# A decoder trunk in fp32: all products of a weight's rounded part first, then those of its remainder

## The chip, the cores and the metric

The kernel runs on one core of one Trainium2 chip. The metric is the device time of the whole program in microseconds (us), as a median over runs; lower is better. All weights come from HBM during the run.

## The reference

A trunk of two decoder layers works on 256 tokens of 2048 features, in float32. In short:

```
for i in 0, 1:
    a = rmsnorm(h, attn_norm[i])
    h = h + (sb_dilated_mixer(a) if i % 2 == 0 else fox_mixer(a))     # q, k, v = a @ w_in; 16 heads of 128; @ w_out
    h = h + conv_ffn(rmsnorm(h, ffn_norm[i]))                          # u = x @ w_up (11264 wide); causal conv of width 3;
                                                                       # (silu(gate) * val) @ w_down
    gate = sigmoid(rmsnorm(h, ple_norm[i]) @ w_ple_gate[i])
    h = h + gate * (p[i] @ w_ple[i])
out = rmsnorm(h, final_norm)
```

Layer 0 mixes with 8 stick-breaking and 8 dilated-window heads, layer 1 with 16 heads with forget gates. Nearly all the arithmetic lies in the products with the weights.

## The kernel before

Features stand on the 128 partitions and tokens in the free dimension: h is a tile of 128 x 16 x 256. TensorE multiplies in a format that keeps fewer bits than float32, so that each operand is split in two: a rounded part and a remainder. An activation tile holds both for a block of 128 features, `act[:, k, 0, :]` and `act[:, k, 1, :]`, 256 columns each. A product of weight and activation is made of three partial products: rounded with rounded, rounded with remainder, remainder with rounded.

Two of them share the weight's rounded part, and are one matmul of 512 columns, called *wide* here: the weight block of 128 x 128 is loaded (LDWEIGHTS, the row PEld of the profile) and both parts of the activation stream through it (L207). The third is a *narrow* matmul of 256 columns with the block of the weight's remainder (L209). The wide one fills `ps[:, j]`, a bank of PSUM with two halves; the narrow one adds to the second half. When all k are done, `joined` (L263, L264) or `add_to_h` adds the halves.

A weight is cut into pieces, four blocks of 128 rows by 256 columns in most. One transfer of the SP queue brings two pieces (L149). ScalarE casts a piece into the rounded part (L165), and VectorE subtracts to get the remainder (L166); a call of `unit` sees to it that three pieces are split ahead of use. The split pieces lie in four buffers w. `gemm_unit` takes one piece: for each half j of its 256 columns and each k it issues wide, narrow, wide, narrow. `gemm_v` does the same for the values v, with the roles of weight and activation exchanged: the activation's block is loaded, and the weight's two parts stream (L242 wide, L244 narrow).

Some products do not follow this pattern: `flat` ones (p @ w_ple, named psp, L203), the values of the first head pair of layer 1 together with its forget gates (L256), and the last pair of gate outputs (L734). They issue narrow products alone, three for each k.

The program is written in the order of the layers: for each of eight pairs of heads the tiles psq, psk and psv; then the output projection (pso); the up projections in pairs (psu) and, in three blocks, the down projection (psd); then the gates (psg). PSUM has two tiles for these. Work of attention, norms and convolution is put among the pieces: `defer` holds it back by a number of pieces. A scheduler then orders each engine's instructions, mostly as written; the engines wait for one another by semaphores. `staggered` lets the first two pairs of outputs wait with their last piece, so that the last activations may come late.

Of the kernel before, what the change touches and what calls it, by code (L numbers as in the profile page):

```python
# [48 lines left out]


def _stagger(pairs):
    """The first two pairs end together, so that their last inputs may come late."""
    a, b = pairs[0], pairs[1]
    return sum([a[:-1], b[:-1], a[-1:], b[-1:]] + pairs[2:], [])

# [3 lines left out]


def _units():
    """Pieces of the weights, in the order in which they are used."""
    full = _cuts(KT)
    ple = [[("w_ple", l, 0, 2, c * 256, 256) for c in range(8)] for l in range(DEPTH)]
    out = list(ple[0])
    for l in range(DEPTH):
        for hp in range(NH // 2):
            if l % 2 == 1 and hp == 0:
                out += [("w_vf", l, k0, kc, 2 * D, 256 + NH) for k0, kc in VF_CUTS]
            for part in range(3):  # L70
                if l % 2 == 0 or hp > 0 or part < 2:
                    out += _pair("w_in", l, part * D + hp * 256, 0, full)
            if l > 0:
                out.append(ple[l][hp])
        out += _stagger([_pair("w_out", l, op * 256, 0, full) for op in range(8)])
        for g0, g1 in BLOCKS:
            for g in range(g0, g1):
                for half in range(2):
                    out += _pair("w_up", l, half * FF + g * 256, 0, full)
            out += _stagger([_pair("w_down", l, op * 256, 2 * g0, _cuts(2 * (g1 - g0))) for op in range(8)])  # L80
        for op in range(8):
            out += _pair("w_ple_gate", l, op * 256, 0, full)
    return out


def _groups(units):
    """Pieces that one transfer brings."""
    out, i = [], 0
    while i < len(units):
        room = 512 if i < 2 else 1024 if i < 12 else 2048  # L90
        n, size = 0, 0
        while i + n < len(units) and size + units[i + n][3] * units[i + n][5] <= room:
            size += units[i + n][3] * units[i + n][5]
            n += 1
        out.append(units[i:i + n])
        i += n
    return out
# [7 lines left out]
def trunk(ctx: ExitStack, tc: tile.TileContext, xT, pT, pos, gains, conv, bf, cst, wst, out):  # L105
    nc = tc.nc
# [30 lines left out]
    def t3_tile(name, shape=(P, 768), dt=F32):  # L137
        return work.tile(list(shape), dt, name=name, tag="t3", bufs=4)

# [1 line left out]
    raws, ready = [], []  # L141
    at = {"group": 0, "off": 0, "unit": 0, "tick": 0, "rows": 0}

# [32 lines left out]
        assert (u[0], u[1], u[2], u[4]) == (kind, l, k0, c0), (u, kind, l, k0, c0)  # L176
        return u[3], w

    # what waits for other engines is given to TensorE some pieces later
    later = []  # L180

    def defer(n, fn):
# [9 lines left out]
            due[0][1]()  # L192

    def gemm_unit(ps, act, kind, l, c0, k0, first, last, koff=0, flat=False):
        """ps[:, j, 0] and ps[:, j, 1] sum to W[:, 128 columns]^T A^T."""
        kc, w = unit(kind, l, k0, c0)
        for j in range(2):
            js = slice(j * P, (j + 1) * P)
            for k in range(kc):
                a = act[:, k0 - koff + k]  # L200
                if flat:
                    for n, (s, t) in enumerate(((0, 0), (0, 1), (1, 0))):
                        nc.tensor.matmul(ps[:, j, 0, :], lhsT=w[:, k, s, js], rhs=a[:, t, :],  # L203
                                         start=first and k == 0 and n == 0,
                                         stop=last and k == kc - 1 and n == 2)
                    continue
                nc.tensor.matmul(ps[:, j], lhsT=w[:, k, 0, js], rhs=a,  # L207
                                 start=first and k == 0, stop=False, skip_group_check=True)
                nc.tensor.matmul(ps[:, j, 1, :], lhsT=w[:, k, 1, js], rhs=a[:, 0, :],  # L209
                                 start=False, stop=last and k == kc - 1, skip_group_check=True)  # L210
        tick()

# [5 lines left out]
            k0 += kc  # L218

    def staggered(name, act, kind, l, cuts, done, k0=0, koff=0):  # L220
        """All pairs of outputs; the first two end together."""
        n = len(cuts)
        ps = [mm_tile(name) for _ in range(2)]
        for part in (range(n - 1), (n - 1,)):
            for op in range(2):
                gemm(ps[op], act, kind, l, op * 256, cuts, k0, koff, part)
                if part == (n - 1,):
                    done(op, ps[op])
        for op in range(2, 8):
            p = mm_tile(name)  # L230
            gemm(p, act, kind, l, op * 256, cuts, k0, koff)
            done(op, p)

    def gemm_v(ps, act, l, c0):
        """ps[:, t, 0] and ps[:, t, 1] sum to A[tokens of tile t] W[:, 256 columns]."""
        for i in range(4):
            kc, w = unit("w_in", l, 4 * i, c0)
            for t in range(2):
                tsl = slice(t * P, (t + 1) * P)
                for k in range(kc):  # L240
                    a = act[:, 4 * i + k]
                    nc.tensor.matmul(ps[:, t], lhsT=a[:, 0, tsl], rhs=w[:, k],  # L242
                                     start=i == 0 and k == 0, stop=False, skip_group_check=True)
                    nc.tensor.matmul(ps[:, t, 1, :], lhsT=a[:, 1, tsl], rhs=w[:, k, 0, :],  # L244
                                     start=False, stop=i == 3 and k == kc - 1, skip_group_check=True)
            tick()

    def gemm_vf(ps, act, l):
        """The same with the columns of the forget gates, all in ps[:, t]."""
        n = 256 + NH  # L250
        for k0, kc in VF_CUTS:
            _, w = unit("w_vf", l, k0, 2 * D)
            for t in range(2):
                for k in range(kc):
                    for i, (a, b) in enumerate(((0, 0), (0, 1), (1, 0))):
                        nc.tensor.matmul(ps[:, t, :n], lhsT=act[:, k0 + k, a, t * P:(t + 1) * P],  # L256
                                         rhs=w[:, k, b, :], start=k0 + k + i == 0,
                                         stop=k0 + k == KT - 1 and i == 2)
            tick()
# [12 lines left out]
        nc.vector.tensor_add(out=hs, in0=hs, in1=t)  # L272

    def parts(dst, src):
        """src as the sum of two parts that TensorE takes whole."""
        nc.scalar.copy(out=dst[:, :, 0, :], in_=src)
        nc.vector.tensor_sub(out=dst[:, :, 1, :], in0=src, in1=dst[:, :, 0, :].bitcast(F32))

# [1 line left out]
    def norm_parts(op, g, dst):  # L280
        """h pair op is final: its parts, with the gains."""
        for j in range(2):
            k = 2 * op + j
            nc.scalar.activation(out=dst[:, k, 0, :], in_=h[:, k, :], func=AF.Copy,
                                 scale=gn[:, g, k:k + 1])
            nc.vector.scalar_tensor_tensor(
                out=dst[:, k, 1, :], in0=h[:, k, :], scalar=gn[:, g, k:k + 1],
                in1=dst[:, k, 0, :].bitcast(F32), op0=ALU.mult, op1=ALU.subtract)
# [8 lines left out]
            nc.vector.tensor_add(out=acc, in0=acc, in1=sq)  # L297

    def norm_sums(more=()):
        """Reciprocal roots of the mean squares, one token a partition."""  # L300
        ps = at_tile("nps")
        nc.vector.tensor_add(out=acc[:, 0, :], in0=acc[:, 0, :], in1=acc[:, 1, :])
        rows = [acc[:, 0, :], *more]
# [18 lines left out]
                                           op0=ALU.add, op1=ALU.mult)  # L322

    def norm_rows(mixer):
        """The same, one token a column, in every partition."""
        dg = t2_tile("nd", (P, 2, P))
        ps = at_tile("rps")
        for t in range(2):
# [18 lines left out]
        defer(5, lambda: norm_rows(mixer))  # L347

    def with_rows(fn):
        """fn reads rb: not before norm_rows."""  # L350
        if at["rows"] > at["tick"]:
            later.append((at["rows"], fn))
        else:
            fn()
# [1 line left out]
    rb2 = rb.unsqueeze(1).to_broadcast([P, 2, S])  # L356
    rq2 = rq.unsqueeze(1).to_broadcast([P, 2, S])

# [1 line left out]
    def load_p(l):  # L360
        raw = t2_tile("pr")
        nc.sync.dma_start(out=raw, in_=pT[:, l])
        return raw

    def ple_up(l, op):
        """A pair of p W_ple, kept until its gates are there."""
        ps = at_tile("psp").rearrange("p j (a s) -> p j a s", a=2) if l > 0 else mm_tile("psp")
        gemm(ps, pact, "w_ple", l, op * 256, (2,), flat=True)
        nc.scalar.copy(out=pl[:, 2 * op:2 * op + 2, :], in_=ps[:, :, 0, :])
# [29 lines left out]
        nc.gpsimd.dma_start(out=bft, in_=bf)  # L399
        nc.gpsimd.dma_start(out=cv, in_=conv)  # L400

# [1 line left out]
    rc = cpool.tile([32, S], F32, name="rc")  # L403
    rs = cpool.tile([32, S], F32, name="rs")

# [30 lines left out]
        nc.vector.tensor_mul(out=x[:32], in0=x[:32], in1=rc.unsqueeze(1).to_broadcast([32, 2, S]))  # L436
        nc.vector.tensor_add(out=x[:32], in0=x[:32], in1=sw)

# [1 line left out]
    def sb_first(q, k):  # L440
        sc = at_tile("scs")
        for j in range(2):
# [75 lines left out]
        return pe, s  # L518

    def sm_second(pe, s):  # L520
        """The weights, one key a partition."""
        sp = at_tile("sps")
        for j in range(2):
            for i in range(3):
# [14 lines left out]
                             skip_group_check=True)  # L539
        parts(dst[:, 2 * hp:2 * hp + 2], av[:, 0, :].rearrange("p (j s) -> p j s", j=2))  # L540

# [1 line left out]
    def forget_gates(l, ps):  # L543
        c2 = cpool.tile([64, S], F32R, name=f"c2_{l}")
        sel = cpool.tile([64, NH], F32R, name=f"sel_{l}")
# [104 lines left out]
        nc.vector.tensor_mul(out=c[0], in0=c[0], in1=c[1])  # L650
        parts(hid[:, 2 * (g - g0):2 * (g - g0) + 2], c[0])

# [1 line left out]
    X, Y = bufs  # L654
    for l in range(DEPTH):
        st = {}
# [179 lines left out]
```

## Time and profile before

| what | value |
|---|---|
| median of 3 runs | 2520.75 us (2520.5 to 2521.31) |
| span of the profiled execution | 2519.2 us |
| TensorE products (PE) | 2497.2 us busy, 14270 instructions |
| weight loads (PEld) | 2173.1 us busy, 14270 instructions |
| VectorE (DVE) | 1716.3 us busy |
| ScalarE (ACT) | 1319.4 us busy |
| read from HBM | 452.86 MB, 181 GB/s over the span |

The profile is of one execution; its span is from the first to the last instruction, and no other time of that execution is given. PE rows are products, PEld rows the loads of their weights, which overlap products. A product's duration in the profile reaches to its modelled end, and neighbours overlap; the distance from one start to the next says what a product costs in a stream. In a row of a group, the number after x counts instructions, then follow busy time in us, the mean of one in ns, and the idle time of the engine just before them. In a row of the timeline stand the start and the duration in us, then engine, line and tiles.

### The profile page before, as it was taken

The numbers are of one execution on the slowest core, as the hardware profiler recorded it, in microseconds if no ns is written. First come the engines' busy times: TensorE is split into PE (matmuls) and PEld (weight loads), VectorE is DVE, ScalarE is ACT, GpSimd is POOL, SyncE is SP. The second block draws the span as 40 slices with busy tenths as digits, with TensorE's granted clock in tenths as the row PEclk, the third lists the DMA queues.
The fourth block names the chain that finished last, engine by engine and source line by source line (L and its number), as shares of the span: only waits on it lengthen the run. The fifth ranks groups of instructions, "written<-read, shape, count | busy, mean of one in ns | idle before, by whom it ended". The sixth has DMA issues, their size and how long they took to land. (4 is left out here: it accounts for less than half of the span.)

```text
span 2519.2 us, 34810 instructions
## 1 busy us (share of the span) xinstructions
PE 2497.2 (99%) x14270; PEld 2173.1 (86%) x14270; DVE 1716.3 (68%) x2386; ACT 1319.4 (52%) x1747; POOL 2.5 (0%) x8
## 2 busy tenths in 40 slices
PE   8999999999999999999999999999999999999997
PEld 7888888888888888888888888888888888888887
DVE  7767667776567657777765555677765776677676
ACT  6554455554455445555554444555544554455564
POOL 0000000000000000000000000000000000000000
PEclk9999999999999999999999999999999999999999
DMA  7444455555555555555454444555555555555553
GB/s 259 167 168 167 167 184 184 185 184 192 183 193 184 180 188 184 190 181 199 170 179 163 163 161 165 183 192 184 187 184 184 187 184 186 193 187 180 182 191 117
DMA packets 66431, 457.20 MB, mean 181 GB/s; under 512 B 7408, under 2 KB 7424, under 8 KB 16608
## 3 DMA queue, kind: packets, MB, share of 16 engines
q1 hardware_dynamic: 66096, 454.53, 50.5%
q8 instruction: 111, 1.82, 0.3%
q0 software_dynamic: 176, 0.46, 0.1%
q14 instruction: 48, 0.39, 0.0%
HBM read 452.86 MB, written 2.10 MB: 181 GB/s over the span
## 5 line engine op out<-in xcount | busy, mean ns | idle before, releaser
L166 DVE TENSOR_TENSOR w<-wr,w 128x1024 fp32r<-128x1024 f32 (+2 forms) x882 | 1049.8, 1191 | 532.3 <-ACT w L165 529.9
L165 ACT CAST w<-wr 128x1024 fp32r<-128x1024 f32 (+2 forms) x882 | 903.4, 1025 | 710.6 <-PE psd L209 186.7
L207 PE MATMUL psu<-act,w 128*128 128x512 f32 x2816 | 995.5, 397 | 0.0
L209 PE MATMUL psu<-act,w 128*128 128x256 f32 x2816 | 791.3, 281 | 0.0
L207 PEld LDWEIGHTS psu<-act,w 128*128 128x128 f32 x2816 | 529.4, 188 | 130.6
L209 PEld LDWEIGHTS psu<-act,w 128*128 128x128 f32 x2816 | 528.6, 188 | 0.0
L207 PE MATMUL psd<-act,w 128*128 128x512 f32 x1408 | 497.8, 397 | 0.0
L209 PE MATMUL psd<-act,w 128*128 128x256 f32 x1408 | 395.6, 281 | 0.0
L207 PEld LDWEIGHTS psd<-act,w 128*128 128x128 f32 x1408 | 264.7, 188 | 65.3
L209 PEld LDWEIGHTS psd<-act,w 128*128 128x128 f32 x1408 | 264.3, 188 | 0.0
L207 PE MATMUL psq<-act,w 128*128 128x512 f32 x512 | 183.9, 400 | 0.0
L207 PE MATMUL psk<-act,w 128*128 128x512 f32 x512 | 182.8, 399 | 0.0
L207 PE MATMUL pso<-act,w 128*128 128x512 f32 x512 | 181.5, 398 | 0.0
L242 PE MATMUL psv<-w,act 128*128 128x512 f32 x480 | 172.5, 399 | 0.7 <-DVE jn L264 0.7
L207 PE MATMUL psg<-act,w 128*128 128x512 f32 x480 | 170.0, 398 | 0.0
L209 PE MATMUL psq<-act,w 128*128 128x256 f32 x512 | 143.9, 281 | 0.7 <-DVE w L166 0.7
L209 PE MATMUL psk<-act,w 128*128 128x256 f32 x512 | 143.9, 281 | 0.0
L209 PE MATMUL pso<-act,w 128*128 128x256 f32 x512 | 143.9, 281 | 0.0
L244 PE MATMUL psv<-w,act 128*128 128x256 f32 x480 | 135.2, 282 | 0.0
L209 PE MATMUL psg<-act,w 128*128 128x256 f32 x480 | 134.9, 281 | 0.0
L263 ACT COPY jn<-psu 128x512 f32<-128x512 f32 x88 | 51.7, 588 | 147.0 <-PE psu L209 147.0
L264 DVE TENSOR_TENSOR jn<-jn,psu 128x512 f32<-128x512 f32 x88 | 60.5, 688 | 93.0 <-ACT jn L263 93.0
(202 smaller groups left out, 2317.0 us busy)
## 6 DMA issues: line engine op xcount, KB each, us to landing
wr<-in_w SPq DMA_DIRECT2D x388, 1024.0 KB, 4.8
wr<-in_w SPq DMA_DIRECT2D x36, 768.0 KB, 4.3
wr<-in_w SPq DMA_DIRECT2D x8, 896.0 KB, 4.6
wr<-in_w SPq DMA_DIRECT2D x7, 512.0 KB, 5.1
h<-in_x SPq DMA_DIRECT2D x4, 512.0 KB, 7.2
out_dram<-h SPq DMA_DIRECT2D x8, 256.0 KB, 2.4
wr<-in_w SPq DMA_DIRECT2D x2, 816.0 KB, 4.7
ct<-in_c SPq DMA_DIRECT2D x1, 841.0 KB, 6.6
```

Of the source, the lines that this page charges most:

```text
L165: nc.scalar.copy(out=w[:, :, 0, :], in_=raw)
L166: nc.vector.tensor_sub(out=w[:, :, 1, :], in0=raw, in1=w[:, :, 0, :].bitcast(F32))
L207: nc.tensor.matmul(ps[:, j], lhsT=w[:, k, 0, js], rhs=a, start=first and k == 0, stop=False, skip_group_check=True)
L209: nc.tensor.matmul(ps[:, j, 1, :], lhsT=w[:, k, 1, js], rhs=a[:, 0, :], start=False, stop=last and k == kc - 1, skip_group_check=True)
L242: nc.tensor.matmul(ps[:, t], lhsT=a[:, 0, tsl], rhs=w[:, k], start=i == 0 and k == 0, stop=False, skip_group_check=True)
L244: nc.tensor.matmul(ps[:, t, 1, :], lhsT=a[:, 1, tsl], rhs=w[:, k, 0, :], start=False, stop=i == 3 and k == kc - 1, skip_group_check=True)
L263: nc.scalar.copy(out=t, in_=ps[:, :, 1, :])
L264: nc.vector.tensor_add(out=t, in0=t, in1=ps[:, :, 0, :])
```

## The change

In `gemm_unit` and in `gemm_v` the loop over k is run twice for each half j of a piece: once for the wide products, once for the narrow ones. Every product stays, with its operands; `start` is still on the first wide product and `stop` on the last narrow one. The flat products keep their order. Comments and docstrings are dropped as well, which moves the lines' numbers by two behind this place.

```diff
         for j in range(2):
             js = slice(j * P, (j + 1) * P)
-            for k in range(kc):
-                a = act[:, k0 - koff + k]
-                if flat:
+            if flat:
+                for k in range(kc):
+                    a = act[:, k0 - koff + k]
                     for n, (s, t) in enumerate(((0, 0), (0, 1), (1, 0))):
...
-                    continue
-                nc.tensor.matmul(ps[:, j], lhsT=w[:, k, 0, js], rhs=a,
+                continue
+            for k in range(kc):
+                nc.tensor.matmul(ps[:, j], lhsT=w[:, k, 0, js], rhs=act[:, k0 - koff + k],
                                  start=first and k == 0, stop=False, skip_group_check=True)
-                nc.tensor.matmul(ps[:, j, 1, :], lhsT=w[:, k, 1, js], rhs=a[:, 0, :],
+            for k in range(kc):
+                nc.tensor.matmul(ps[:, j, 1, :], lhsT=w[:, k, 1, js], rhs=act[:, k0 - koff + k, 0, :],
                                  start=False, stop=last and k == kc - 1, skip_group_check=True)
...
                 for k in range(kc):
-                    a = act[:, 4 * i + k]
-                    nc.tensor.matmul(ps[:, t], lhsT=a[:, 0, tsl], rhs=w[:, k],
+                    nc.tensor.matmul(ps[:, t], lhsT=act[:, 4 * i + k, 0, tsl], rhs=w[:, k],
                                      start=i == 0 and k == 0, stop=False, skip_group_check=True)
-                    nc.tensor.matmul(ps[:, t, 1, :], lhsT=a[:, 1, tsl], rhs=w[:, k, 0, :],
+                for k in range(kc):
+                    nc.tensor.matmul(ps[:, t, 1, :], lhsT=act[:, 4 * i + k, 1, tsl], rhs=w[:, k, 0, :],
                                      start=False, stop=i == 3 and k == kc - 1, skip_group_check=True)
```

On TensorE, one half (128 columns) of a piece of the first query projection (psq) stood like this before, wide and narrow in turn; the numbers behind the names are those of buffers, and the waits are for ScalarE's rounded part and VectorE's remainder:

```order
L207 MATMUL psq_289<-act0_68,w_313 128x512 [waits Activation_49]
L209 MATMUL psq_289<-act0_68,w_313 128x256 [waits DVE_49]
L207 MATMUL psq_289<-act0_68,w_313 128x512
L209 MATMUL psq_289<-act0_68,w_313 128x256
L207 MATMUL psq_289<-act0_68,w_313 128x512
L209 MATMUL psq_289<-act0_68,w_313 128x256
L207 MATMUL psq_289<-act0_68,w_313 128x512
L209 MATMUL psq_289<-act0_68,w_313 128x256
```

The same piece, both halves, with the change:

```order
L208 MATMUL psq_289<-act0_68,w_313 128x512 [waits Activation_49]
L208 MATMUL psq_289<-act0_68,w_313 128x512 x3
L211 MATMUL psq_289<-act0_68,w_313 128x256 [waits DVE_49]
L211 MATMUL psq_289<-act0_68,w_313 128x256 x3
L208 MATMUL psq_289<-act0_68,w_313 128x512 x4
L211 MATMUL psq_289<-act0_68,w_313 128x256 x4
```

The wait for the remainder (DVE) has moved behind three more wide products.

At the start of the program the order of VectorE is touched too, around the first head pair, where the factors of the first norm (rT, then rb and rq) are made for the sums of psq and psk (jn). Before:

```order
L321 SCALAR_TENSOR_TENSOR rT<-nt,ny 128x2 [waits DVE_49]
L166 TENSOR_TENSOR w<-wr,w 128x4x256 [waits Activation_49]
L329 TENSOR_SCALAR nd<-ct,rT 128x128 [waits DVE_49]
L329 TENSOR_SCALAR nd<-ct,rT 128x128
L337 TENSOR_TENSOR ndl<-nd,ndh 128x256 [waits Activation_49]
L340 COPY rb<-rps 128x256 [waits PE_49]
L166 TENSOR_TENSOR w<-wr,w 128x4x256 [waits DMAHW2_49,Activation_49]
L342 TENSOR_SCALAR rq<-rb 128x256 [waits DVE_49]
L264 TENSOR_TENSOR jn<-jn,psq 128x512 [waits Activation_49]
```

With the change:

```order
L323 SCALAR_TENSOR_TENSOR rT<-nt,ny 128x2 [waits DVE_49]
L331 TENSOR_SCALAR nd<-ct,rT 128x128 [waits DVE_49]
L331 TENSOR_SCALAR nd<-ct,rT 128x128
L166 TENSOR_TENSOR w<-wr,w 128x4x256 [waits DMAHW2_49,Activation_49]
L339 TENSOR_TENSOR ndl<-nd,ndh 128x256 [waits Activation_49]
L266 TENSOR_TENSOR jn<-jn,psq 128x512 [waits Activation_49]
L342 COPY rb<-rps 128x256 [waits PE_49]
L266 TENSOR_TENSOR jn<-jn,psk 128x512 [waits Activation_49]
L344 TENSOR_SCALAR rq<-rb 128x256 [waits DVE_49]
```

The first of the two splits (L166) has moved up into the chain that makes rT, the second stands ahead of ndl, and the sum of psq is now made before rb and rq. TensorE's own product for rb (rps, L339 before, L341 now) has moved towards the end of psk. Outside this stretch the other engines' orders are unchanged.

## The prediction

> **What bounds the kernel now.** I read the page's busy table first, then its costliest groups, then the waits of TensorE, then the timeline of a steady stretch.
>
> ```profile
> span 2519.2 us, 34810 instructions
> PE 2497.2 (99%) x14270; PEld 2173.1 (86%) x14270; DVE 1716.3 (68%) x2386; ACT 1319.4 (52%) x1747; POOL 2.5 (0%) x8
> PEclk9999999999999999999999999999999999999999
> L207 PE MATMUL psu<-act,w 128*128 128x512 f32 x2816 | 995.5, 397 | 0.0
> L209 PE MATMUL psu<-act,w 128*128 128x256 f32 x2816 | 791.3, 281 | 0.0
> L207 PEld LDWEIGHTS psu<-act,w 128*128 128x128 f32 x2816 | 529.4, 188 | 130.6
> ...
> L242 PE MATMUL psv<-w,act 128*128 128x512 f32 x480 | 172.5, 399 | 0.7 <-DVE jn L264 0.7
> ```
>
> TensorE is busy for 99% of the span at full granted clock, and the two products of the large weights (L207, wide, 512 columns; L209, narrow, 256 columns) show no idle time ahead of them. Nothing but TensorE's own pace sets the end. What it does wait for is short, and all at the two ends of the program:
>
> ```profile
> PE psp L203 <- ACT w L165: 5.9, 2, 5.4
> PE rps L331 <- DVE nd L329: 2.7, 1, 2.7
> PE nps L306 <- DVE sq L745: 1.6, 1, 1.6
> PE psp L203 <- ACT pl L369: 1.4, 2, 1.3
> PE psq L209 <- DVE w L166: 0.7, 1, 0.7
> PE psv L242 <- DVE jn L264: 0.7, 1, 0.7
> ```
>
> These are microseconds in total, times, and the longest. Only the last two, 0.7 us each, touch lines that the change touches. So the question is what a step of TensorE takes from one start to the next, not the modelled durations of 397 and 281 ns, which overlap. The timeline shows the starts:
>
> ```profile
> 999.83 0.40 PE L207 MATMUL psu<-act,w 128*128 128x512 f32 x1
> 1000.07 0.28 PE L209 MATMUL psu<-act,w 128*128 128x256 f32 x1
> 1000.07 0.19 PEld L207 LDWEIGHTS psu<-act,w 128*128 128x128 f32 x1
> 1000.18 0.40 PE L207 MATMUL psu<-act,w 128*128 128x512 f32 x1
> ...
> 1007.96 0.40 PE L207 MATMUL psu<-act,w 128*128 128x512 f32 x1
> ```
>
> From 999.83 to 1007.96 there are 23 pairs of a wide and a narrow product: 8.13 / 23 = 0.3535 us a pair. Within a pair about 0.235 us go from the wide to the narrow one and 0.118 from the narrow to the next wide one: 0.46 ns a column in both. The pairs number 2816 + 1408 + 3 x 512 + 480 = 6240 (psu, psd, psq, psk, pso, psg) and 480 of psv: 6720 x 0.3535 = 2376 us of the 2519.
>
> **The change, part by part.** No product, load, byte or column is added or removed. In each half piece four pairs become four wide products and then four narrow ones. So of every four wide-to-narrow steps three become wide-to-wide, and of every four narrow-to-wide steps three become narrow-to-narrow. Over the program that is 0.75 x 6720 = 5040 steps of each new kind. A nanosecond on one of them is 5 us, which is also 0.2% of 2520.75 us, about what a measurement of this kernel can tell from no change. Everything hangs on these two prices.
>
> Narrow to narrow is in the trace. The last pair of gate outputs (L734) is two runs of 48 narrow products each, and the input projection of layer 1 (psp, L203) has runs of 12:
>
> ```profile
> 2492.20 5.65 PE pse L734 x48
> 2497.86 5.67 PE psg L734 x48
> 1290.53 1.41 PE psp L203 x12
> 1332.91 1.36 PE psp L203 x12
> ```
>
> These rows are from the chain of waits (start, us). 5.65 / 48 = 0.1177 and 5.67 / 48 = 0.1181 us a step: what narrow-to-wide takes. The psp runs give 0.1175 and 0.1133. I take 0.1177 against 0.118: 5040 x -0.0003 = -1.5 us. Bounds: 0.1181 (+0.5 us) and 0.1133 (5040 x -0.0047 = -24 us).
>
> Wide to wide is not in the trace. The nearest rows say whether a wide product's 0.235 us is its own or due to the narrow one behind it. It can be read where something else follows:
>
> ```profile
> 36.86 0.40 PE L207 MATMUL psk<-act,w 128*128 128x512 f32 x1
> 37.09 0.48 PE L306 MATMUL nps<-ct,acc 128*128 128x2 f32 x3
> ...
> 423.07 0.28 PE L209 MATMUL psu<-act,w 128*128 128x256 f32 x1
> 423.07 0.53 PEld L306 LDWEIGHTS nps<-ct,acc 128*128 128x128 f32 x4
> 423.19 0.50 PE L306 MATMUL nps<-ct,acc 128*128 128x2 f32 x4
> 423.52 0.19 PEld L207 LDWEIGHTS psu<-act,w 128*128 128x128 f32 x1
> ```
>
> Behind a wide product a product of two columns starts 0.23 us later, and behind a narrow one 0.12 us later: the same as in the pairs. So the time belongs to the product in front and its columns, whatever follows, and I take 0.235 us for wide to wide: 0 us. Bounds: twice the fastest narrow step, 2 x 0.1133 = 0.2267 (5040 x -0.0083 = -42 us), and, upwards, 1 ns a step for what no row shows (+5 us).
>
> Do the weights come in time? In the pairs a load starts with the product ahead of it and is recorded for 188 ns, longer than a narrow step; so loads overlap one another, and what counts is how close they can follow. The rows at 423.07 show four loads and then the next at 423.52: 0.45 / 4 = 0.112 us a load, below 0.118. Four narrow products in a row ask for one load each 0.118 us, so the loads stay hidden; if they did not, see the second rival.
>
> A rule of the Trainium skill gives smaller steps. "TensorE: Matmul & The Clock Gate", section "Back-to-back issue gap", puts an isolated step at N / 2.4 + 2.5 ns: 216 and 109 ns, 325 a pair. The trace has 353.5 and disagrees by 28 ns; an estimate by that page for both kinds of new step is 5040 x (-19 - 9) ns = -141 us. That would be right only if alternating were what costs the 28 ns, and the runs of L734 speak against it for the narrow half.
>
> The rest of a piece keeps its dates. Each half piece still ends with the narrow product of its last k, so its sum is ready and its weight buffer free when they were. The activations of the later k are read earlier by up to 3 x 0.118 = 0.35 us. The closest case that I found is the last head pair of layer 0, whose remainder is written just ahead of its use in the output projection:
>
> ```profile
> 339.50 0.68 DVE L277 TENSOR_TENSOR act<-avp,act 128x512 fp32r<-128x512 f32 x1
> 341.21 0.40 PE L207 MATMUL pso<-act,w 128*128 128x512 f32 x1
> ```
>
> It is done at 340.18; the piece starts at 341.21 and needs it from its third k on, 2 x 0.353 later before and 2 x 0.235 later now: 1.5 us of lead are left of 1.7. Cost 0; without that cover it would be 0.24 us, once.
>
> **The start.** Two waits move. The first is for a late remainder of a weight:
>
> ```profile
> 28.85 0.40 PE L207 MATMUL psq<-act,w 128*128 128x512 f32 x1
> 29.94 0.38 PE L209 MATMUL psq<-act,w 128*128 128x256 f32 x1 [0.69 <-DVE w L166]
> ...
> 47.47 0.28 PE L209 MATMUL psk<-act,w 128*128 128x256 f32 x1
> 48.41 0.47 PE L242 MATMUL psv<-w,act 128*128 128x512 f32 x1 [0.66 <-DVE jn L264]
> ```
>
> The step from 28.85 takes 1.09 us instead of 0.235, 0.85 too long. Three wide products now go in between, 0.70 us, so 0.15 us of the wait is left. The second, at 48.41 (0.94 instead of 0.118, 0.82 too long), is for the sum of psq, which VectorE joins only after the row factors rb. In the new order VectorE joins psq ahead of rb and rq, but the chain that makes rT and nd, which stands ahead of it, has one split of a weight (L166, 1.2 us) put into it. Queued behind the join are rb, rq and the join of psk, none of which TensorE needs before the scores of this head pair, 16 pairs on. What the first wait gives back, TensorE arrives earlier here, so I do not add them: the two together are worth between -1.7 us (both gone) and +0.8 us (the second grows by one split, about 1.2 us, while the first gives 0.4). I take -0.5.
>
> **Sum.** -1.5 + 0 + 0 - 0.5 = -2 us on the profiled span of 2519.2 us; the median of the runs, 2520.75, lies 1.6 us above that span, and I carry this difference over: 2518.75, say 2519 us.
>
> **Rivals.** *Alternating costs something* (faster). Going from one width to the other disturbs the stream, and runs of one width go at the pace of the fastest psp run. Price: -24 - 42 = -66 us, 2455 us. For it: that run, at 0.1133. Against it: L734 keeps 0.1177 over 96 products of one width, another psp run 0.1175, and a wide product takes 0.23 us in front of a two-column one. By the page's formula it would be the 2380 us of the estimate above. It decides from 1 ns a step. Chance 0.14, most of it between the ends.
>
> *The weight loads bind in the narrow half* (slower). In pairs a load behind a narrow product is followed by a long wide one in which the loads catch up; four narrow ones in a row have no such rest. If loads of different blocks cannot follow closer than, say, 0.125 us, a narrow step grows by 7 ns: 5040 x 0.007 = +35 us, 2556 us; if each took its recorded 188 ns, 5040 x 0.070 = +353 us, 2874 us. For it: in L734 two of three neighbouring loads bring the same block, so that run does not prove the pace for different blocks. Against it: the 0.112 us of L306. It decides from a load pace above 0.118. Chance 0.09.
>
> *The scheduler undoes it.* The built order shows the grouping in every piece, so this is out, but for the products of the attention and norms, which stand among the pieces as before.
>
> **How the numbers follow.** No measurable change: 0.77, with its own range of 2515.7 to 2523. Faster 0.14, slower 0.09. The range must hold 0.8, so it takes in the near part of both rivals: 2509 (a gain of 2 ns on each wide-to-wide step) to 2529 (2 ns lost on each narrow step).
>
> **What would show it.** In the timeline of the changed kernel eight products of a half piece should take 1.41 us from the first wide one to the first wide one of the next half, with wide starts 0.235 and narrow starts 0.118 us apart. PEld should stay without waits that hold TensorE. The wait of psq's first narrow product for w should shrink to 0.2 us or vanish. A wide step of 0.23 or less, or a narrow one above 0.12, proves the forecast wrong, and the size gives the time at 5 us a nanosecond.

## The result and the profile after

The changed kernel takes 2477.5 us (median of 4 runs, 2476.15 to 2478.58) against 2520.62 us before. The ratio is 0.983 with a 95% interval of 0.981 to 0.984: 43 us or 1.7% faster. The forecast was 2519 us, no measurable change, with a range of 2509 to 2529.

The page of the changed kernel, its busy table and the groups that answer to those shown of before (L208 is the wide product now, L211 the narrow one):

```profile
span 2474.4 us, 34810 instructions
PE 2453.4 (99%) x14270; PEld 2145.1 (87%) x14270; DVE 1715.1 (69%) x2386; ACT 1320.2 (53%) x1747; POOL 2.5 (0%) x8
PEclk9999999999999999999999999999999999999998
L208 PE MATMUL psu<-act,w 128*128 128x512 f32 x2816 | 767.9, 394 | 0.0
L211 PE MATMUL psu<-act,w 128*128 128x256 f32 x2816 | 437.3, 277 | 0.0
```

Instructions, granted clock and the share of TensorE are as before, and the products still have no idle time ahead of them. TensorE does the same products in less time. One stretch of the up and down projections of layer 0, 600 to 700 us, by TensorE's instructions in it, first before, then after (us, busy, in brackets the count, clock, DMA share, GB/s):

```profile
600.00:700.00 100.00, 100.00 (x568) 1.00 0.53 190
```

```profile
600.00:700.00 100.00, 100.00 (x579) 1.00 0.53 189
```

579 against 568 products in the same time is 1.9% more, in a stretch that waits for nothing. The timeline after, start and duration in us:

```profile
1000.85 1.09 PE L208 MATMUL psu<-act,w 128*128 128x512 f32 x4
1001.78 0.62 PE L211 MATMUL psu<-act,w 128*128 128x256 f32 x4
1002.24 0.62 PE L208 MATMUL psu<-act,w 128*128 128x512 f32 x2
```

From the first wide product of one half piece to that of the next go 1.39 us, 0.93 for the wide and 0.46 for the narrow ones. Before, four pairs took 4 x 0.3535 = 1.41 us. The starts of the products with the large weights in the two traces give the steps; some fifty in each kernel are longer than 260 ns and are left out:

| step from one start to the next, mean ns | before | after |
|---|---|---|
| wide to wide | none | 230.9 |
| wide to narrow | 234.8 | 235.1 |
| narrow to narrow | 117.8 (94 steps, the two runs of L734 alone) | 115.3 |
| narrow to wide | 118.5 | 113.7 |

In most half pieces of the changed kernel, those of four blocks in `gemm_unit`, the four wide steps are near 226, 236, 231 and 236 ns, and the four narrow ones 118.5 and three times 113.4. Four pairs were 4 x 353.3 = 1413 ns and are 1387: 26 ns, 1680 times, is 44 us. That accounts for the gain. The start gives about 1 us: the step that waits for the late remainder takes 0.49 us where it took 1.09, and the one that waits for psq's sum 0.47 where it took 0.94. The first wait is gone from the list of waits, and the second has shrunk from 0.7 us to this:

```profile
PE psv L243 <- DVE jn L266: 0.2, 1, 0.2
```

One place shows more than the sum. The last pair of gate outputs (L734 before, L736 now) was not touched. Its two runs of 48 narrow products, in the chain of waits after:

```profile
2447.77 5.44 PE pse L736 x48
2453.21 5.46 PE psg L736 x48
```

They took 5.65 and 5.67 us before. The same instructions on the same tiles in the same order step at 113.3 ns where they stepped at 117.7, and only what ran ahead of them differs. So a narrow product has no price of its own here: there is a *fast pace*, 113.3 ns for 256 columns, and a *slow pace*, 117.7. The experiments ask what moves the stream from one to the other. "Lines of pse" below means these two runs: they tell at which pace the stream was left.

### The profile page after: what moved, and what is told of

It reads as the page before. It is cut to its first block, busy times and chain, and to the rows that moved or that the text cites. A ratio compares the mean times of both kernels' runs of the same rounds, so it can differ in the third digit from the quotient of the medians.

```text
span 2474.4 us, 34810 instructions
## 1 busy us (share of the span) xinstructions
PE 2453.4 (99%) x14270; PEld 2145.1 (87%) x14270; DVE 1715.1 (69%) x2386; ACT 1320.2 (53%) x1747; POOL 2.5 (0%) x8
## 5 line engine op out<-in xcount | busy, mean ns | idle before, releaser
L166 DVE TENSOR_TENSOR w<-wr,w 128x1024 fp32r<-128x1024 f32 (+2 forms) x882 | 1049.2, 1191 | 500.0 <-ACT w L165 497.8
L208 PE MATMUL psu<-act,w 128*128 128x512 f32 x2816 | 767.9, 394 | 0.0
L208 PEld LDWEIGHTS psu<-act,w 128*128 128x128 f32 x2816 | 476.7, 188 | 59.9
L211 PEld LDWEIGHTS psu<-act,w 128*128 128x128 f32 x2816 | 428.2, 188 | 63.8
L211 PE MATMUL psu<-act,w 128*128 128x256 f32 x2816 | 437.3, 277 | 0.0
L208 PE MATMUL psd<-act,w 128*128 128x512 f32 x1408 | 388.8, 394 | 0.0
L208 PEld LDWEIGHTS psd<-act,w 128*128 128x128 f32 x1408 | 236.4, 188 | 26.7
L211 PEld LDWEIGHTS psd<-act,w 128*128 128x128 f32 x1408 | 219.1, 188 | 34.7
L211 PE MATMUL psd<-act,w 128*128 128x256 f32 x1408 | 224.6, 278 | 0.0
L208 PE MATMUL psq<-act,w 128*128 128x512 f32 x512 | 141.6, 398 | 0.0
L208 PE MATMUL psk<-act,w 128*128 128x512 f32 x512 | 140.9, 396 | 0.0
L208 PE MATMUL pso<-act,w 128*128 128x512 f32 x512 | 140.0, 395 | 0.0
L208 PE MATMUL psg<-act,w 128*128 128x512 f32 x480 | 131.1, 395 | 0.0
L208 PEld LDWEIGHTS psq<-act,w 128*128 128x128 f32 x512 | 86.9, 188 | 11.5 <-issue 0.2
L208 PEld LDWEIGHTS psk<-act,w 128*128 128x128 f32 x512 | 86.8, 188 | 11.2
L208 PEld LDWEIGHTS pso<-act,w 128*128 128x128 f32 x512 | 86.7, 188 | 11.0
L243 PEld LDWEIGHTS psv<-w,act 128*128 128x128 f32 x480 | 81.7, 188 | 11.8 <-PE psk L211 0.4
L208 PEld LDWEIGHTS psg<-act,w 128*128 128x128 f32 x480 | 81.3, 188 | 10.2
```

Source lines behind the costliest of these rows:

```text
L166: nc.vector.tensor_sub(out=w[:, :, 1, :], in0=raw, in1=w[:, :, 0, :].bitcast(F32))
L208: nc.tensor.matmul(ps[:, j], lhsT=w[:, k, 0, js], rhs=act[:, k0 - koff + k], start=first and k == 0, stop=False, skip_group_check=True)
L211: nc.tensor.matmul(ps[:, j, 1, :], lhsT=w[:, k, 1, js], rhs=act[:, k0 - koff + k, 0, :], start=False, stop=last and k == kc - 1, skip_grou ...
L243: nc.tensor.matmul(ps[:, t], lhsT=act[:, 4 * i + k, 0, tsl], rhs=w[:, k], start=i == 0 and k == 0, stop=False, skip_group_check=True)
```

## The experiments

All kernels start from the kernel before, unless another is named, and all edits are made in `gemm_unit` and `gemm_v` alike where the text doesn't say otherwise; the diffs show `gemm_unit`, and brackets in them stand for code that is left out. Times of single runs are set beside the run of before on the same chip.

**Does the gain follow the number of changes of width? e1_groups2, e2_groups8.** Groups of two, and of eight.

```diff
+            for ka in range(0, kc, 2):                 # e1_groups2
+                for k in range(ka, min(ka + 2, kc)):
                     (wide product of k)
+                for k in range(ka, min(ka + 2, kc)):
                     (narrow product of k)
```

```diff
+            for j in range(2):                         # e2_groups8
+                for k in range(kc):
                     (wide product of j, k)
+            for j in range(2):
+                for k in range(kc):
                     (narrow product of j, k)
```

> Groups of two: wide, wide, narrow, narrow for each two k, in both gemm_unit and gemm_v. A theory 'changes of width cost': the trace of before has 353.3 ns a pair with one wide-narrow-wide change per pair, the changed kernel 346.8 ns with a quarter; on a straight line that is 344.6 + 8.7 ns per change, so half a change per pair gives 349.0 ns a pair, 29 us under before: 2491 us. Theory 'addresses' (a product costs more when its neighbour reads the same activation block): no neighbours of the same k are left, so all of the gain is there: 2477 us. Theory 'two paces' (a stream locks onto 113.3 or 117.8 ns per 256 columns by its history): anything from 2455 to 2520, not on the line.

> Groups of eight: both halves' wide products of a piece, then both halves' narrow ones. 'Changes of width cost': an eighth of a change per pair, 345.7 ns, 51 us under before: 2469 us. 'Addresses': as the changed kernel, 2477 us. 'Two paces': between 2430 and 2520; the second half of a wide run repeats the steps of the first half (about 231 ns on average), then also near 2477 us.

Measured: 2480.05 and 2478.85 us, before 2520.23. Groups of two, four (2477.5) and eight lie within 2.6 us of one another; the straight line over the number of changes, which asked for 2491 and 2469, falls. The timeline of groups of two and of eight:

```profile
1000.32 0.62 PE L209 MATMUL psu<-act,w 128*128 128x512 f32 x2
1000.78 0.39 PE L212 MATMUL psu<-act,w 128*128 128x256 f32 x2
1001.02 0.62 PE L209 MATMUL psu<-act,w 128*128 128x512 f32 x2
```

```profile
1001.02 2.02 PE L211 MATMUL psu<-act,w 128*128 128x512 f32 x8
1002.88 1.07 PE L216 MATMUL psu<-act,w 128*128 128x256 f32 x8
1003.79 1.56 PE L211 MATMUL psu<-act,w 128*128 128x512 f32 x6
```

In groups of two, two pairs take 0.70 us; the steps are 226, 236, 118.5, 113.4. In groups of eight 16 products take 2.77 us, 0.346 a pair. The wide run goes 226, 236, 231, 236, 230.5, 236, 231, 236, and the narrow one 118.5 and seven times 113.4. So a longer run saves on narrow products (only the first is slow) and loses the same on wide ones (only the first is fast).

**Is it the neighbour that reads the same activation block? e3_shift.**

```diff
             for k in range(kc):
+                m = (k + kc // 2) % kc
                 (wide product of k)
-                (narrow product of k)
+                (narrow product of m)
```

> Wide and narrow in turn as before, but each narrow product is of another k than the wide one ahead of it (k shifted by half a piece). Same number of changes of width as before, but no neighbours that read the same activation block. 'Changes of width cost' and 'two paces' (same sequence of lengths): 353.3 ns a pair, 2520 us. 'Addresses': the gain of the change, about 2477 us.

Measured: 2522.87 us, before 2520.23; wide steps of 235 and narrow ones of 118.4 ns, 5.65 us in the lines of pse. The shared block is out: wide and narrow in turn are as slow where neighbours read different blocks.

**No wide products at all. e4_allnarrow, e8_allnarrow_timed.**

```diff
-                nc.tensor.matmul(ps[:, j], lhsT=w[:, k, 0, js], rhs=a, ...)
+                nc.tensor.matmul(ps[:, j, 0, :], lhsT=w[:, k, 0, js], rhs=a[:, 0, :], ...)
+                nc.tensor.matmul(ps[:, j, 1, :], lhsT=w[:, k, 0, js], rhs=a[:, 1, :], ...)
                 (narrow product of k)
```

> Every wide product is made as two narrow ones, so that all products with the large weights are narrow, three for each k; 6720 products and loads more, no change of width. 'Changes of width cost': three steps of 113.3 ns, 340 ns for what a pair did, 90 us under before: 2431 us. 'Addresses' (neighbours of one k are back): three steps of 117.8 ns, 353.4: 2520 us. 'Two paces': either of the two, or a mixture. If the loads bind, more than 2520 us.

> The kernel of e4_allnarrow again, timed in three rounds: 2439.7 us in one run, so a ratio of 0.968 to before and 0.985 to the changed kernel; the interval should exclude both 1 and the changed kernel's 0.983.

Measured: 2439.7 us in one run, and 2437.9 us (2437.21 to 2439.72) when timed, before 2520.37: ratio 0.967, interval 0.966 to 0.969. It beats both kernels. The page of e4_allnarrow, and TensorE's instructions in the stretch from 600 to 700 us:

```profile
span 2437.9 us, 48251 instructions
PE 2415.5 (99%) x20990; PEld 2402.3 (99%) x20990; DVE 1715.4 (70%) x2386; ACT 1323.8 (54%) x1747; POOL 2.5 (0%) x8
...
600.00:700.00 100.00, 100.00 (x884) 1.00 0.54 191
```

100 us / 884 = 113.1 ns a step. Three of them are 340 ns for what a pair did in 353.3. It issues 6720 products and loads more, the loads are busy for 99% of the span, and it is still the fastest. These products write the same halves of PSUM in the same order as the kernel before and read the same blocks. So what is slow in the kernel before is neither the blocks nor the halves of PSUM: it comes with the 512 columns in one instruction, between narrow products.

**What a wide product costs in a run of its own kind. e5_allwide.**

```diff
-                nc.tensor.matmul(ps[:, j, 1, :], lhsT=w[:, k, 1, js], rhs=a[:, 0, :], ...)
+                nc.tensor.matmul(ps[:, j], lhsT=w[:, k, 1, js], rhs=a, ...)
```

> The narrow product of the weight's remainder is made wide too (it takes both parts of the activation, so the product of the two remainders is added to the sum): wide products only, two for each k, as many loads as before. Theory 'a wide product behind a wide one pays' (runs of eight showed 231 and 236 ns in turn): 233.4 ns a step, 467 ns a pair, 763 us over before: 3283 us. Theory 'only a change of width pays': 226.7 ns a step, 453 ns a pair, 3194 us.

Measured: 3277.7 us. The steps are 233.1 ns on average, in places 231 and 236 in turn, in places 233 throughout. A wide product among its like costs 6.4 ns more than two narrow ones at the fast pace, and 1.7 ns less than in turn with narrow ones. Behind such a run the lines of pse are fast (5.45).

**Do the loads do it? e6_load64, e11_narrow64.** In `gemm_unit` alone, wide and narrow in turn, and all narrow:

```diff
+                m = P if (first and k == 0) or (last and k == kc - 1) else P // 2
+                ms = slice(j * P, j * P + m)
-                nc.tensor.matmul(ps[:, j], lhsT=w[:, k, 0, js], rhs=a, ...)
+                nc.tensor.matmul(ps[:m, j], lhsT=w[:, k, 0, ms], rhs=a, ...)
                 (the other products likewise)
```

> Wide and narrow in turn as before, but in gemm_unit all products except the first and the last of a sum load and fill only 64 of the weight block's 128 columns (half of each output's features are left out there); the streams keep their 512 and 256 columns. If the loads take time from the streams or hold them up, the pair falls from 353.3 towards 340 ns (three times the best 113.3) or below: 73 us under before or more, 2448 us or less. If the streams set the pace alone, 353.3 ns and 2520 us.

> All products narrow as in e4_allnarrow, but in gemm_unit all except the first and the last k of a sum load and fill only 64 of the weight block's 128 columns (half of each output's features are left out there). If the loads bind the narrow run, the step falls below 113.3 ns, to what the stream of 256 columns takes by itself: 108 to 110 ns, about 2360 to 2390 us. If the stream binds, 113.3 ns and 2440 us.

Measured: 2483.58 us in turn, before 2519.65, and 2443.54 us all narrow, before 2520.37. The loads of half the columns, in the kernel with both widths in turn:

```profile
1000.07 0.19 PEld L211 LDWEIGHTS psu<-act,w 128*128 128x128 f32 x1
1000.30 0.14 PEld L209 LDWEIGHTS psu<-act,w 128*64 128x64 f32 x1
1000.42 0.13 PEld L211 LDWEIGHTS psu<-act,w 128*64 128x64 f32 x1
```

In turn, the wide step falls from 235 to 228 ns and the narrow one stays at 119: neither of the two theories' numbers, but what the edit shortens does have a part in what a wide product costs. It has one in the pace too. The lines of pse behind this order, in the chain of waits of e6_load64, are fast:

```profile
2455.22 5.44 PE pse L736 x48
2460.66 5.46 PE psg L736 x48
```

So with loads of 64 columns, wide and narrow in turn do not leave the stream on the slow pace: 228 and 119 ns are close to what the first wide and the first narrow product of a group take (226 and 118.5). The edit halves the loads and, with them, the partitions of PSUM that are filled; no run tells the two apart.

All narrow, the step stays at 113.3 ns: at the fast pace the load does not set it. A load falls from 188 to 134 ns, 54 ns for 64 columns; the Trainium skill, "TensorE: Matmul & The Clock Gate", section "LDWEIGHTS (loading the stationary operand)", counts a column as 1 / 1.2 ns, 53 ns for 64, and the trace agrees in this difference. By the same rule a whole load of 128 columns is an estimated 107 ns, and the rows have 188.

**And how close can loads follow? e7_third128.** From e4_allnarrow, in `gemm_unit`:

```diff
-                (third product, 256 columns)
+                c = S if last and k == kc - 1 else S // 2
+                nc.tensor.matmul(ps[:, j, 1, :c], lhsT=w[:, k, 1, js], rhs=act[:, k0 - koff + k, 0, :c], ...)
```

> All products narrow as in e4_allnarrow, but in gemm_unit the third one, of the weight's remainder, takes only 128 of 256 columns (the rest of that product is left out, except in the last k). If the step of 113.3 ns in a narrow run is the pace of the loads, the third step stays near 112 ns: about 2432 us. If it is the pace of the stream, it falls to 57 ns: about 2110 us.

Measured: 2492.28 us, more than with the whole product. Both theories missed:

```profile
1000.04 0.34 PE L208 MATMUL psu<-act,w 128*128 128x256 f32 x1
1000.21 0.28 PE L210 MATMUL psu<-act,w 128*128 128x256 f32 x1
1000.33 0.22 PE L213 MATMUL psu<-act,w 128*128 128x128 f32 x1
1000.39 0.33 PE L208 MATMUL psu<-act,w 128*128 128x256 f32 x1
```

The short step takes 0.06 us, as the theory of the stream had it, but the step behind it 0.17. The loads in the same stretch:

```profile
1000.22 0.19 PEld L213 LDWEIGHTS psu<-act,w 128*128 128x128 f32 x1
1000.33 0.19 PEld L208 LDWEIGHTS psu<-act,w 128*128 128x128 f32 x1
1000.44 0.19 PEld L210 LDWEIGHTS psu<-act,w 128*128 128x128 f32 x1
1000.56 0.19 PEld L213 LDWEIGHTS psu<-act,w 128*128 128x128 f32 x1
```

They start 0.11 to 0.12 us apart, also where the short product stands between, so that what it saves is lost again in the next step. That this step waits for a load is read from the distances; no wait is recorded. Three loads take 0.346 us, 0.115 each. So the narrow run at 113.3 ns is near the closest spacing of loads of 128 columns seen here (0.108 us at the least in this stream of psu), and a shorter stream buys nothing. The lines of pse are slow (5.65) behind this order.

**Is the pace handed on? e10_one_pair.** The grouped order in one pair of gate outputs only:

```diff
+            if kind == "w_ple_gate" and l == 1 and c0 == 6 * 256:
+                (all wide products of the half piece, then all narrow ones)
+                continue
```

> The kernel before, with the grouped order only in the pair of gate outputs of layer 1 that stands ahead of the last two runs of 48 narrow products. Time: 1.3 us less at most, 2519 us. What it is for is the pace of those runs: 117.8 ns a step in before (5.65 us for 48), 113.3 in the changed kernel (5.44), by the same instructions. Theory 'the pace is handed on by what ran ahead': 113.3, 5.44 us. Theory 'the pace comes from the run itself, or from its place': 117.8, 5.65 us.

Measured: 2519.65 us, as before on that chip. The lines of pse:

```profile
2490.84 5.44 PE pse L742 x48
2496.28 5.46 PE psg L742 x48
```

Fast. The pace is handed on: 64 products in the grouped order, right ahead, and 96 untouched narrow products behind them go at 113.3 ns instead of 117.7, to the last one.

**What puts the stream on the slow pace, and what brings it back? e9_every_second, e12_one_wide, e13_two_wide.** All narrow, but with a wide product left in every second k, in the first k of a half piece, and in the first two k together:

```diff
             for k in range(kc):                        # from e4_allnarrow
+                if k % 2 == 0:                         # e12_one_wide: if k == 0
+                    (wide product of k)
+                else:
                     (two narrow products of k in its place)
                 (narrow product of the remainder of k)
```

```diff
+            for k in (0, 1):                           # e13_two_wide
+                (wide product of k)
+            for k in (0, 1):
+                (narrow product of the remainder of k)
+            for k in range(2, kc):
                 (three narrow products of k)
```

> For every second k the wide product is made as two narrow ones, so that each wide product stands between narrow ones: wide, narrow, narrow, narrow, narrow. Theory 'the pace is handed on': a wide product behind narrow ones at the fast pace takes 226.5 ns, the narrow one behind it 118.4, the other three 113.4 each: 685 ns for two pairs' work, 2448 us. Theory 'every change of width costs alike' (13.3 ns in before for wide-narrow-wide): 2 x 340 + 13.3 = 693 ns, 2476 us.

> In each half piece only the first k keeps its wide product; the other k have three narrow ones: one wide and ten narrow products in a row (for four k). Theory 'a lone wide product puts the stream on the slow pace, and narrow ones keep what they find': 235.3 + 10 x 117.7 = 1412 ns a half piece, 2517 us. Theory 'a wide product costs some nanoseconds near it only': 4 x 340 + 13 = 1373 ns, 2452 us.

> In each half piece the first two k have wide, wide, narrow, narrow, the other two three narrow products each: two wide and eight narrow in a row. Theory 'two wide products in a row bring the stream back to the fast pace': 226 + 236 + 118.4 + 7 x 113.4 = 1374 ns a half piece, 2456 us. Theory 'any wide product among narrow ones spoils them': 2 x 235.5 + 8 x 117.7 = 1413 ns, 2518 us.

Measured: 2516.98 us (before 2520.37), 2518.66 us (before 2523.9) and 2460.78 us (the same before). One wide product and ten narrow ones, the first and last rows of a half piece of e12_one_wide:

```profile
1000.29 0.40 PE L209 MATMUL psu<-act,w 128*128 128x512 f32 x1
1000.53 0.28 PE L216 MATMUL psu<-act,w 128*128 128x256 f32 x1
...
1001.71 0.40 PE L209 MATMUL psu<-act,w 128*128 128x512 f32 x1
```

Two wide products and eight narrow ones, e13_two_wide:

```profile
1000.00 0.62 PE L208 MATMUL psu<-act,w 128*128 128x512 f32 x2
1000.46 0.40 PE L211 MATMUL psu<-act,w 128*128 128x256 f32 x2
...
1001.37 0.62 PE L208 MATMUL psu<-act,w 128*128 128x512 f32 x2
```

1.42 us against 1.37, for the same columns. With a lone wide product all ten narrow ones behind it step at 117.7 ns and the wide one at 235; with two in a row the wide ones take 226 and 236, the first narrow one 118.5 and the seven others 113.4. The lines of pse are 5.65 us behind e9_every_second and e12_one_wide, 5.44 behind e13_two_wide. e9_every_second missed both its numbers: I had expected the narrow products to recover behind a lone wide one.

What follows for the streams of `gemm_unit` with loads of 128 columns: at the fast pace a first wide product still takes 226 ns, twice 113.3. Lone ones among narrow products leave the stream on the slow pace, and the narrow products behind them (ten in e12_one_wide, 96 in before) do not leave it. Two, four, six or eight wide ones in a row leave it slow for one narrow product and fast from the second on.

Three in a row do not always. The down projection has 128 half pieces of three blocks, and the trace of the changed kernel shows two of them one after the other:

```profile
834.35 0.85 PE L208 MATMUL psd<-act,w 128*128 128x512 f32 x3
835.04 0.52 PE L211 MATMUL psd<-act,w 128*128 128x256 f32 x3
835.39 0.86 PE L208 MATMUL psd<-act,w 128*128 128x512 f32 x3
836.09 0.51 PE L211 MATMUL psd<-act,w 128*128 128x256 f32 x3
836.43 1.09 PE L208 MATMUL psd<-act,w 128*128 128x512 f32 x4
```

The wide steps of the first are 226, 236 and 231 ns, and all three narrow ones stay slow (118, 117, 118). Those of the second, which finds the slow pace, are 231, 229 and 236, and its narrow ones 118, 113 and 114. All 128 are of one kind or the other, 64 of each.

Nor is it the widths alone. In the values (`gemm_v`) of the changed kernel, behind four wide products, the steps between the narrow ones are all slow in 62 of 120 half pieces and all fast in the other 58. And where the values end and psp begins, the pace changes with no wide product between, in the chain of waits of the changed kernel:

```profile
1307.91 0.46 PE psv L246 x4
1308.37 1.41 PE psp L203 x12
```

Four narrow products in 0.46 us are at the fast pace, twelve in 1.41 at the slow one. So that narrow products keep a pace is shown for the runs of pse and for the half pieces of `gemm_unit`, and not across every seam; the rule of even groups holds for `gemm_unit`. The runs show this much; they don't show what inside TensorE keeps the pace. That it lies in how loads and streams meet, as e6_load64 suggests, is argued and not shown.

## Why the prediction was wrong

*The bound* was right: TensorE's own pace sets the end, and it still does, at 99% busy with no waits between.

*Narrow to narrow* was the first step that failed. The prediction had both paces in front of it, 0.1177 and 0.1181 in the runs of L734 and 0.1133 in a run of psp, took the first, called it "what narrow-to-wide takes", and held its 96 products against the other. (The eight runs of psp in layer 1 of that trace are of both kinds: three take 1.41 or 1.42 us, three 1.36 and two 1.39.) The runs of L734 stood behind a stream in turn and had been handed its slow pace, as e10_one_pair shows. Three of four narrow steps now go at about 113.4. Narrow to narrow gave 118.5 - 115.3 = 3.2 ns a step, 5040 x 3.2 = 16 us, where 1.5 was taken and 24 was the bound. The steps from narrow to wide, which the sum left as they were, gave another 1680 x 4.8 = 8 us. (Counted with the half pieces of three blocks there are 5008 and 1712 of these steps, which changes no term by more than 0.2 us.)

*Wide to wide* failed by its reason. That a two-column product starts 0.23 us behind a wide one shows what a follower does, and says nothing on what went ahead: in those rows, too, a lone narrow product stood in front. Measured: 230.9 ns against 234.8, 5040 x 3.9 = 20 us, about half of the bound of -42 us. The wide step at the head of a run does reach that bound's 226.7 (226), the others don't.

*The loads* stay hidden, as said, though with little to spare, as the loads of e7_third128 show (0.115 us each against steps of 0.1133).

*The start* came out better than forecast. The first step, expected to be 0.15 us too long where it was 0.85, is 0.25 too long, and the second 0.35 where it was 0.82. Together they gave 1.1 us where 0.5 was taken, within the bounds of -1.7 and +0.8. The lead of the last activations held: no wait at the output projection.

*The rivals.* "Alternating costs something" had 0.14 and is what happened: runs of one width go at the pace of the fast psp run, for most of the narrow products, and it was priced at 66 us where 43 came, the wide ones being the difference. Its evidence against was the two runs of L734, the very ones that carried the slow pace along. The 109 and 216 ns for a bare step that the Trainium skill works with ("TensorE: Matmul & The Clock Gate", section "Back-to-back issue gap") were not met in any steady stretch: the smallest were 113.3 and 226, and the measurement decides. The rival of loads that bind did not occur, and all narrow, with half as many loads again, is faster still.

## What to carry to other kernels

A step read from a trace is the step in its surroundings. Where one instruction shows two prices in one trace, as narrow products did here (0.1133 and 0.1177), neither is a constant: find what went ahead of each before taking one into a sum over thousands of steps.

Where a stream of products mixes 512 and 256 columns in this format, don't leave single wide ones between narrow ones: two in a row are enough for most of the gain (2480 us for groups of two, 2477.5 for four), three can leave the narrow ones behind them slow, and splitting each wide one into two narrow ones was better than either (2437.9 us), in spite of the loads it adds. A run of untouched products behind a changed place can show what a change did to the stream, though the place itself is too short to time.

## What the runs showed of the hardware that was not expected

- The step of the same 256-column product is 113.3 or 117.7 ns at the same granted clock (0.997 and 0.998 over the two executions), and 96 products in a row keep the pace that they are handed (5.44 or 5.65 us for 48).
- One product of 512 columns among ten of 256 makes all ten slow (1.42 us a half piece); two in a row do not (1.37 us); three in a row do in 64 of 128 half pieces.
- With loads of 64 columns for 128, and half of the partitions of PSUM filled, single products of 512 columns between those of 256 leave the stream fast (5.44 us for 48 behind it).
- A product of 512 columns steps in 226 ns at the head of a run at the fast pace, in 235 alone between narrow ones, and in 233.1 on average in a run of its like.
- A product of 128 columns steps in 0.06 us, but the next step then takes 0.17, so that it saves nothing where loads of 128 columns start 0.11 to 0.12 us apart.
